# Moving weight sums from GpSimd to VectorE and fetching a stage's raw weights eight deep, in a one-core transformer layer

## The chip, the cores and the metric

The kernel runs on one core of one Trainium2 chip. The metric is the device time of one execution in microseconds (us). The kernel before took 2723.49 us (median of three runs, 2721.57 to 2726.60).

## The reference

One layer over 1024 latent tokens and 256 context tokens, model width 1024, all in fp32:

```python
def ffn_sublayer(h, shift, scale, gate, g, w_in, w_out):
    hn = modulate(rmsnorm(h, g), shift, scale)
    a, b = jnp.split(hn @ w_in, 2, axis=-1)
    y = (jax.nn.silu(a) * b) @ w_out
    return h + 0.5 * gate[:, None, :] * y

# reference(), in its order
h = x + grid_pos_emb(rows)[None];  hc = ctx
mods   = jnp.split(jax.nn.silu(c) @ w_ada + b_ada, 9, axis=-1)
mods_c = jnp.split(jax.nn.silu(c_ctx)[None] @ w_ada + b_ada, 9, axis=-1)
h  = ffn_sublayer(h,  mods[0],   mods[1],   mods[2],   g_ffn1, w_ffn1_in, w_ffn1_out)
hc = ffn_sublayer(hc, mods_c[0], mods_c[1], mods_c[2], g_ffn1, w_ffn1_in, w_ffn1_out)
p_lat = project(h,  mods[3],   mods[4],   g_mix, w_in, PROJ_SIZES)     # q k v gates | o u vs ga gb
p_ctx = project(hc, mods_c[3], mods_c[4], g_mix, w_in, PROJ_SIZES[:4]) # q k v gates
# short convolution and silu on q, k; chunked mLSTM in both directions, started from the context's states
y_lat = merge_branches(p_lat[4:], hlf + hlb, ...)                      # w_branch_a, w_branch_b, w_out
h = h + mods[5][:, None, :] * y_lat
h = ffn_sublayer(h, mods[6], mods[7], mods[8], g_ffn2, w_ffn2_in, w_ffn2_out)
return rmsnorm(h, g_final)
```

The feed-forward width is 2816, so `w_ffn1_in` has 5632 columns: 44 blocks of 128.

## The kernel before

**Products.** Every fp32 operand of a large product is split into a high and a low part: ScalarE casts it to the TensorE's fp32r format (line 145), VectorE subtracts the cast from the original (line 146), and TensorE does three products (high by high, high by low, low by high). So each weight page goes from DRAM to a raw page, through one cast and one subtraction, into a page of pairs, `hl` or `ring`.

**Products with sums.** For the 1024 latent tokens a 2 x 2 block of products is done as seven products of sums and differences of the blocks. The weights' sums are made just before the cast, on the raw page, by one 128x512 addition or subtraction each. Before the change they are done on GpSimd (`G`), in three places: `Pair.load` (lines 1215, 1217, 1218, 1220; 24 pairs of 128 weight columns, four sums each), `Rows.load` (lines 1152 to 1158; 32 sums) and `Stage.preload` through `Gate.presum` (lines 358 and 359; 12 sums for the first three column blocks of each feed-forward's first half).

**Stages**, by the time of the profile: the conditioning's modulation (`adr`, line 827, until 43 us); the context tokens' first half of the first feed-forward ("context stage", 43 to 202, products `pa` and `pb` through `proj` and line 172); the same for latents (the "Gate", `qa` and `qb`, line 396, from 202 to some 650) and its second half (`po`, line 522); the context's second half; then the projections: value rows (`Rows`), k pairs and q pairs (line 1252, 1030 to 1225), the sigmoid pairs for o, ga and gb (1225 to 1470), and so on to the branches, their output and the second feed-forward.

**The context stage.** `Weights` hands out the 44 split pages in order. A page's load is one step: its DMA into one of two `raw` buffers, and its split into one of three `hl` buffers. `W.done()` after each product of 24 matmuls starts the next load. Meanwhile the latents are prepared: addition of the position embedding (`add_pos`, line 876), sums of squares (`Norm.sq`, lines 198 and 199), scaling by the norm (`Norm.inplace`, lines 248 and 249) and the first split factors of the latents (`fa` in `Factors.early`, `fb` and the subtraction of line 295). After each pair of products the gated result is formed and stored (`sil`, `gc`, lines 946 to 950).

**What sets the order.** The program records its operations in the order it is written, and a scheduler of the language then sets each engine's order. The code steers this with a queue `todo` of small steps, which `pump` takes between matmuls: 512 columns of matmul buy one step, less the step's `cost`. A step marked `later` waits, and all behind it, until VectorE's account (`debt`, filled by `dv` with an estimated length of each VectorE operation, and paid off by matmul columns) is below 128. All DMAs of the kernel are issued by SP, in order. In the projections a `Stream` keeps at least four split `ring` pages ahead of TensorE.

**The pairs.** `Pair.load(p)` for p = 1 takes two of four raw pages and starts their DMAs. Each later p does its sums on them in place and hands the page to the cast. The seven products go in the order 1, 7, 2, 4, 5, 6, 3; product 7's result is copied to SBUF by ScalarE as `py` (line 1263), product 1's as `px` (line 1258). For q and k, the convolution's taps are VectorE's lines 1331 and 1333 (tile `cv`), and ScalarE's lines 1330 and 1353. During the sigmoid pairs VectorE also computes the remaining modulation vectors (`adacc`, lines 766 and 768), from weights that come through two buffers `adapg` (DMAs of line 756).

Of the kernel before, what the change touches and what calls it, by code (L numbers as in the profile page):

```python
# [56 lines left out]
def _build(ctx, tc, nc, a, out):  # L57
# [48 lines left out]
    class Weights:  # L106


        def __init__(self, order, name):
            self.c = ExitStack()  # L110
            self.pool = self.c.enter_context(tc.tile_pool(name=name, bufs=1, reuse_waits="tile"))
            self.order = deque(order)
            self.ready = deque()
            self.held = 0

        def load(self):
            n, i, w = self.order.popleft()
            src = a[n][i]
# [5 lines left out]
            self.held += 1  # L124

        def take(self, n, i):
            if not self.ready:
                self.load()
# [56 lines left out]
    class Norm:  # L185
# [5 lines left out]
        def sq(self, d, first=None):  # L191
            nt = self.nt
            if d == 0 if first is None else first:
                self.acc = t2("acc")
                S.activation(self.acc[:, :nt], self.h[d], AF.Square)
            else:
                sq = t2("sq")
                S.activation(sq[:, :nt], self.h[d], AF.Square)
                (self.eng if d % self.alt == 0 else V).tensor_tensor(self.acc[:, :nt], self.acc[:, :nt], sq[:, :nt], ALU.add)
# [46 lines left out]
        def inplace(self, d, sc, sh):  # L246
            t = self.h[d]
            V.scalar_tensor_tensor(t, t, sc[:, d:d + 1], self.rb, ALU.mult, ALU.mult)
            S.activation(t, t, AF.Identity, bias=sh[:, d:d + 1])
# [69 lines left out]
    class Gate:  # L319
# [31 lines left out]
        def presum(self, f, eng):  # L351
# [3 lines left out]
            if eng is V:  # L355
                dv()
                dv()
            eng.tensor_tensor(s1, b1, b2, ALU.add)
            eng.tensor_tensor(b1, a1, b1, ALU.subtract)

        def load(self):
# [4 lines left out]
            else:  # L366
# [4 lines left out]
                if p in (5, 6) and "s1" not in s:  # L371
                    self.presum(f, V)
# [200 lines left out]
    class Stage:  # L573
# [284 lines left out]
    W = Weights([("w1i", f, 1024) for f in range(2 * NF)], "w1")  # L858
# [10 lines left out]
    def add_pos(tb, d):  # L869
        hv = h[tb][d].rearrange("p (r c) -> p r c", c=64)  # L870
# [9 lines left out]
    W.load()  # L880
    W.load()
    apg.append(ada_pages(2))
    W.load()
# [25 lines left out]

    n1 = [Norm(h[tb], 512, V) for tb in range(2)]  # L910
    s0, b0 = smod[:, 0, 0, :], mods[:, 0, 0, :]

    def slow(fn, *args, cost=1024):
        f = it(fn, *args)
        f.cost = cost
        todo.append(f)

    for f in range(NF):
# [15 lines left out]
        if f == 12:  # L934
            A.head()
        if f > 12:
            A.preload()
        wa = W.take("w1i", 2 * f)
# [3 lines left out]
        W.done()  # L942
        proj(pb, wb, hnc)
        W.done()
        sil = t2("sil")[:, :256]
        S.activation(sil, pa, AF.Silu)
        V.tensor_mul(sil, sil, pb)
        g = t2("gc", F32R, (128, 2, 256))
        split(g, sil)
        nc.sync.dma_start(gcsp[f // 2, :, f % 2], g.bitcast(F32))  # L950
# [24 lines left out]
    A.gate(A.F.late(fpage, lambda k: []), tick)  # L975
# [153 lines left out]
    class Rows:  # L1129
# [13 lines left out]
        def load(self, p, k):  # L1143
# [57 lines left out]
    class Pair:  # L1201


        def __init__(self, name, i, emit, ctx_emit=None):
            self.name, self.i, self.emit, self.ctx_emit = name, i, emit, ctx_emit
            self.steps = PSEQ if ctx_emit is None else PSEQ[:1] + (8,) + PSEQ[1:]

        def load(self, p):
            if p == 1:
                self.s = [rawpg() for _ in range(2)]  # L1210
                for j in range(2):
                    nc.sync.dma_start(self.s[j], a[self.name][self.i + j])
            a1, a2, b1, b2 = (self.s[j][:, o * 512:(o + 1) * 512] for j in range(2) for o in range(2))
            if p == 7:
                G.tensor_tensor(b1, a1, b1, ALU.subtract)
            elif p == 5:
                G.tensor_tensor(b2, b2, b1, ALU.subtract)  # L1217
                G.tensor_tensor(a1, a1, b2, ALU.add)  # L1218
            elif p == 3:
                G.tensor_tensor(a2, a2, b2, ALU.subtract)  # L1220
# [66 lines left out]

    def pair_steps(*args):
        pr = Pair(*args)
        for p in pr.steps:  # L1290
# [365 lines left out]

    nvs, barvs = rows_steps("wvs", emit_vs)
# [437 lines left out]
```

## Time and profile before

| | us |
|---|---|
| median of three runs | 2723.49 |
| the profiled execution | 2722.22 |
| span of its trace | 2720.4 |
| TensorE busy | 2661.8 |
| VectorE busy | 1974.2 |
| ScalarE busy | 1085.2 |
| GpSimd busy | 330.0 |

One execution is profiled; its span runs from the first to the last instruction, and its own time is 1.8 us longer. In the rows below, PE is TensorE, PEld its weight loads, DVE VectorE, ACT ScalarE, POOL GpSimd, and SPq the DMA queue of SP. L146 is line 146 of the kernel before. "x24" counts instructions. In the timeline the columns are start, length, engine, line, operation, output and inputs, with the idle time just before and what ended it in brackets. A wait reads: engine, line and tile that waited, what it waited for, total us, times, longest. A group of instructions reads: busy us and mean ns of one, then the idle time before them.

### The profile page before, as it was taken

Reading aid. Unit: us, or ns where it says so; the run is one execution under the profiler, and the core shown is the slowest. Engines: PE = TensorE matmul, PEld = TensorE weight load, DVE = VectorE, ACT = ScalarE, POOL = GpSimd, SP = SyncE. Lnnn points to the kernel's source line nnn. Section 1 sums busy time; section 2 is a strip of 40 time slices with the busy share of each in tenths; the row PEclk is TensorE's granted clock in tenths of the full one; section 3 lists DMA queues with packets and bytes.
Section 4 is the critical chain, followed back from the end, with each engine's and each line's share of the span. In section 5 each row is a group of like instructions: output and inputs, shape, how many; then the busy total and the mean of one; then the engine's idle time right before and its main releaser. Section 6 shows DMA issues by size and latency. Waiting matters only on the chain.

```text
span 2720.4 us, 35602 instructions
## 1 busy us (share of the span) xinstructions
PE 2661.8 (98%) x12734; PEld 2210.9 (81%) x12734; DVE 1974.2 (73%) x3469; ACT 1085.2 (40%) x1862; POOL 330.0 (12%) x354
## 2 busy tenths in 40 slices
PE   8899999999999999999999999999999999999998
PEld 4788888888889878777878888888877888888887
DVE  4787897887969646667665677768468977776755
ACT  3564333334436625444434333112145433333432
POOL 0100000000000122232221315443010000000000
PEclk9999999999999999999999999999999999999999
DMA  8862453449668322237554357547331333337645
GB/s 279 283 192 74 162 173 123 145 151 321 212 215 283 123 78 73 87 109 237 172 171 155 106 187 259 191 168 258 125 132 63 128 136 117 123 121 257 198 159 170
DMA packets 199584, 456.73 MB, mean 168 GB/s; under 512 B 20592, under 2 KB 49008, under 8 KB 199408
## 3 DMA queue, kind: packets, MB, share of 16 engines
q1 hardware_dynamic: 199408, 454.47, 49.7%
q8 instruction: 100, 1.64, 0.2%
q14 instruction: 76, 0.62, 0.1%
HBM read 328.95 MB, written 125.51 MB: 167 GB/s over the span
## 4 chain that ended last, share of the span: by engine, by line
PE 52%; DVE 5%; issue 2%; POOL 1%; DMA 1%; ACT 1%; SPq 0%; POOLq 0%; DVEq 0%; ACTq 0%
PE pq L1252 13%; PE qb L396 10%; PE pt L1720 9%; PE po L522 6%; PE qa L396 5%; PE pr L1171 3%; PE pn L1833 2%; PE pu L1560 2%; PE pn L1831 1%; DVE ring L146 1%; PE pkc L1232 1%; DMA adapg<-in_w_ada_dram 1%; PE pm L1677 1%; POOL rawq L1217 0%; POOL rawq L1218 0%
## 5 line engine op out<-in xcount | busy, mean ns | idle before, releaser
L145 ACT CAST ring<-rawq 128x512 fp32r<-128x512 f32 x432 | 266.6, 620 | 565.5 <-PE qb L396 193.4
L146 DVE TENSOR_TENSOR ring<-rawq,ring 128x512 fp32r<-128x512 f32 x432 | 311.1, 722 | 185.9 <-ACT ring L145 183.6
L522 PE MATMUL po<-gring,wring 128*128 128x512 f32 (+1 forms) x1896 | 425.4, 385 | 0.4 <-ACT wring L145 0.3
L522 PEld LDWEIGHTS po<-gring,wring 128*128 128x128 f32 x1896 | 349.4, 188 | 72.2 <-issue 1.2
L396 PE MATMUL qb<-fc,ring 128*128 128x512 f32 x1440 | 340.0, 390 | 1.1 <-DVE u L417 0.8
L396 PEld LDWEIGHTS qb<-fc,ring 128*128 128x128 f32 x1440 | 269.8, 188 | 58.9 <-DVE u L417 2.3
L396 PE MATMUL qa<-fa,ring 128*128 128x512 f32 x1056 | 253.3, 390 | 0.5 <-ACT ring L145 0.5
L396 PEld LDWEIGHTS qa<-fa,ring 128*128 128x128 f32 x1056 | 197.9, 188 | 42.7 <-ACT ring L145 0.9
L1252 PE MATMUL pq<-fc,ring 128*128 128x512 f32 x864 | 216.4, 399 | 14.4 <-ACT py L1263 9.3
L396 PE MATMUL qb<-fb,ring 128*128 128x512 f32 x984 | 229.8, 389 | 0.0
L396 PEld LDWEIGHTS qb<-fb,ring 128*128 128x128 f32 x984 | 184.6, 188 | 38.4 <-DVE fb L146 0.2
L1252 PEld LDWEIGHTS pq<-fc,ring 128*128 128x128 f32 x864 | 162.1, 190 | 52.3 <-ACT py L1263 11.2
L145 ACT CAST wring<-rw 128x512 fp32r<-128x512 f32 x154 | 95.8, 622 | 227.6 <-PE po L522 192.8
L1720 PE MATMUL pt<-yp,ring 128*128 128x512 f32 x768 | 184.2, 396 | 0.0
L146 DVE TENSOR_TENSOR wring<-rw,wring 128x512 fp32r<-128x512 f32 x154 | 105.6, 686 | 94.2 <-ACT wring L145 94.0
L1720 PEld LDWEIGHTS pt<-yp,ring 128*128 128x128 f32 x768 | 144.1, 188 | 29.3
L1252 PE MATMUL pq<-fa,ring 128*128 128x512 f32 x576 | 142.6, 396 | 0.2 <-ACT px L1258 0.2
L1252 PE MATMUL pq<-fb,ring 128*128 128x512 f32 x576 | 137.6, 393 | 0.4 <-DVE mods L783 0.4
L1252 PEld LDWEIGHTS pq<-fa,ring 128*128 128x128 f32 x576 | 108.5, 191 | 24.2 <-ACT px L1258 1.1
L1252 PEld LDWEIGHTS pq<-fb,ring 128*128 128x128 f32 x576 | 107.7, 188 | 23.1 <-PE pu L1601 0.7
L768 DVE SCALAR_TENSOR_TENSOR adacc<-adapg,sc,adacc 128x512 f32<-128x512 f32 x140 | 110.6, 803 | 14.4 <-DMA adapg<-in_w_ada_dram 13.5
L145 ACT CAST ring<-rawt 128x512 fp32r<-128x512 f32 x64 | 39.5, 619 | 186.3 <-PE pt L1720 172.4
(341 smaller groups left out, 4241.8 us busy)
## 6 DMA issues: line engine op xcount, KB each, us to landing
adapg<-in_w_ada_dram SPq DMA_DIRECT2D x144, 256.0 KB, 4.0
fsp<-fhl SPq DMA_DIRECT2D x66, 512.0 KB, 2.7
gring<-fsp SPq DMA_DIRECT2D x66, 512.0 KB, 3.8
raw<-in_w1i_dram SPq DMA_DIRECT2D x44, 512.0 KB, 4.4
graw<-fsp SPq DMA_DIRECT2D x88, 256.0 KB, 3.6
rawq<-in_w1i_dram SPq DMA_DIRECT2D x38, 512.0 KB, 4.2
rawq<-in_w2i_dram SPq DMA_DIRECT2D x38, 512.0 KB, 3.3
fsp<-x SPq DMA_DIRECT2D x66, 256.0 KB, 2.0
```

The source lines that it names most:

```text
L145: S.copy(hl[:, 0, :], src)
L146: V.tensor_sub(hl[:, 1, :], src, hl[:, 0, :].bitcast(F32))
L396: T.matmul(pt, hl[:, x, sl], pages[p][k][:, y, :], start=first and i == 0, stop=i == 11, skip_group_check=not first)
L522: T.matmul(pt[:, cs], w[:, x, sl], g[:, y, cs], start=grp and kp == 0 and i == 0, stop=kp == NFP - 1 and i == 2, skip_group_check=not grp)
L768: eng.scalar_tensor_tensor(acc, pgt, sc2[:, q, k:k + 1], acc, ALU.mult, ALU.add)
L1171: T.matmul(self.pt[m], pg[:, x, sl], hl[:, y, :], start=first and k == 0 and i == 0, stop=k == 3 and i == 2, skip_group_check=not first)
L1232: T.matmul(self.cp[:, o:o + 256], hl[:, x, k * 128:(k + 1) * 128], hnc[kc][:, y, :], start=p == 1 and k == 0 and i == 0, stop=p in (2, 4) ...
L1252: T.matmul(pt, hl[:, x, k * 128:(k + 1) * 128], pg[k][:, y, :], start=first and k == 0 and i == 0, stop=k == 3 and i == 2, skip_group_chec ...
L1560: T.matmul(pu[:, 0:257], ksl[:, kt * 128:(kt + 1) * 128], wv, start=True, stop=True)
L1677: T.matmul(pm[:, n * 128:(n + 1) * 128], vnp_[:, half * 4 + n, :], wsr_[:, half * 4 + n, :], start=True, stop=True)
L1720: T.matmul(pt, hl[:, x, k * 128:(k + 1) * 128], pg[:, y, :], start=kh + k + i == 0, stop=kh == 1 and k == 3 and i == 2)
L1833: T.matmul(pn[:, 0:257], qi[:, c_, :], self.C[d][:, c_, :], start=False, stop=c_ == 1)
```

## The change

1. **Sums.** All 140 sums of `Pair.load`, `Rows.load` and `presum` go from GpSimd to VectorE. `preload` no longer does the `presum` at once but puts it into `todo`, as `later`, at cost 512.
2. **Pairs' pages.** A pair starts the DMAs of the next pair's raw pages at its own third step, instead of at the next pair's first.
3. **Context weights.** Fetching and splitting are taken apart. Raw pages come from the pool `hn`, eight deep (`wraw`; the first four, of which one is new ahead of the last modulation page, from another pool); split pages `hl` are four deep instead of three.
4. **Gated results.** `gate_c` of a column block is recorded after the next block's first product instead of right behind its own.
5. **Latents' preparation.** The steps `add_pos`, `sq`, `inplace` and `early` cost 512 instead of 1024, are `later`, and charge VectorE's account. Twelve empty steps stand between the norm's root and its use. The scaling of the second half of the latents (eight `inplace`) goes to the Gate's list of steps.
6. **First ring pages.** The Gate's first three ring pages are loaded before the context stage's last two products.

```diff
         def load(self):
-            n, i, w = self.order.popleft()
-            raw = self.pool.tile([128, w], F32, name="raw", tag="raw", bufs=2)
-            nc.sync.dma_start(raw, src)
-            hl = self.pool.tile([128, 2, w], F32R, name="hl", tag="hl", bufs=3)
+            n, i, raw = self.raws.popleft()
+            hl = self.pool.tile([128, 2, 1024], F32R, name="hl", tag="hl", bufs=self.depth)
             split(hl, raw)
             self.ready.append((n, i, hl))
...
+        def fetch(self, page):
+            n, i, w = self.order.popleft()
+            raw = page()
+            nc.sync.dma_start(raw, a[n][i])
+            self.raws.append((n, i, raw))
...
-        def done(self, n=1):
-            self.held -= n
-            while self.order and self.held < 3:
+        def done(self, page):
+            if self.raws:
                 self.load()
+            while self.order and len(self.raws) < self.ahead:
+                self.fetch(page)
...
                 if i:
-                    self.q.presum(f, G)
+                    fn = it(self.q.presum, f)
+                    fn.cost, fn.later = 512, True
+                    todo.append(fn)
...
-    W = Weights([("w1i", f, 1024) for f in range(2 * NF)], "w1")
+    W = Weights([("w1i", f, 1024) for f in range(2 * NF)], "w1", 4, 8)
...
+    def wraw():
+        return hnp.tile([128, 1024], F32, name="wraw", tag="pg1", bufs=8)
...
+    for _ in range(W.ahead):
+        W.fetch(wraw)
...
-                slow(add_pos, tb, f - 2)
-                slow(n1[tb].sq, f - 2)
+                slow(add_pos, tb, f - 2, cost=512, later=True)
+                slow(n1[tb].sq, f - 2, cost=512, later=True)
...
-            todo.extend([n1[0].rstd, nop, n1[1].rstd, nop, n1[0].bcast, n1[1].bcast])
+            todo.extend([n1[0].rstd, n1[1].rstd] + [nop] * 12 + [n1[0].bcast, n1[1].bcast] + [nop] * 4)
             for d in range(NKT):
-                slow(n1[0].inplace, d, s0, b0)
-                slow(A.F.early, fpage, 1 if d < 4 else 2, d % 4)
-            for d in range(NKT):
-                slow(n1[1].inplace, d, s0, b0)
+                slow(n1[0].inplace, d, s0, b0, cost=512, later=True)
+                slow(A.F.early, fpage, 1 if d < 4 else 2, d % 4, cost=512, later=True)
...
+        if f == NF - 1:
+            A.q.ring = lambda: hnpage(1, "ring0")
+            for _ in range(HEAD):
+                A.q.load()
+            A.q.ring = A.ring
...
         proj(pa, wa, hnc)
-        W.done()
+        if gated is not None:
+            gated()
+        W.done(wraw)
         proj(pb, wb, hnc)
-        W.done()
+        W.done(wraw)
+        gated = it(gate_c, f, pa, pb)
...
-    A.gate(A.F.late(fpage, lambda k: []), tick)
+    A.gate(A.F.late(fpage, lambda k: [it(n1[1].inplace, k, s0, b0)]), tick)
...
             if p == 1:
-                self.s = [rawpg() for _ in range(2)]
+                self.fetch()
+            elif p == self.steps[2] and self.next is not None:
+                self.next.fetch()
...
             if p == 7:
-                G.tensor_tensor(b1, a1, b1, ALU.subtract)
+                V.tensor_tensor(b1, a1, b1, ALU.subtract)
             elif p == 5:
-                G.tensor_tensor(b2, b2, b1, ALU.subtract)
-                G.tensor_tensor(a1, a1, b2, ALU.add)
+                V.tensor_tensor(b2, b2, b1, ALU.subtract)
+                V.tensor_tensor(a1, a1, b2, ALU.add)
             elif p == 3:
-                G.tensor_tensor(a2, a2, b2, ALU.subtract)
+                V.tensor_tensor(a2, a2, b2, ALU.subtract)
```

Apart from the context stage, TensorE's order is the same but for one swap of small products. Three places show how other engines' orders change. The changed kernel has other line numbers: its cast and subtraction are lines 149 and 150.

The first place is SP's queue at the head of the context stage. `raw` and `wraw` are pages of the first feed-forward's weights, `h` the latents' pages, `hsp` and `gcsp` stores. Before:

```order
L120 DMA raw<-in_w1i_dram 128x1024
L820 DMA adapg<-in_w_ada_dram 128x2x256 x8
L885 DMA cst<-in_cst_dram 128x512
L886 DMA pos<-in_pos_dram 128x320
L921 DMA h<-in_xT_dram 128x512 x2
L120 DMA raw<-in_w1i_dram 128x1024 x2
L921 DMA h<-in_xT_dram 128x512 x4
L855 DMA hsp<-h 128x512
```

Now:

```order
L122 DMA wraw<-in_w1i_dram 128x1024 x2
L827 DMA adapg<-in_w_ada_dram 128x2x256 x8
L903 DMA cst<-in_cst_dram 128x512
L904 DMA pos<-in_pos_dram 128x320
L122 DMA wraw<-in_w1i_dram 128x1024 x8
L951 DMA h<-in_xT_dram 128x512 x2
L122 DMA wraw<-in_w1i_dram 128x1024 x2
L951 DMA h<-in_xT_dram 128x512 x2
```

One more weight page stands ahead of the last modulation page, and eight more ahead of the latents' first pages.

The second place is ScalarE's queue over one q pair (`cv` the convolution's tile; `px`, `py` and `pre` copies out of PSUM; `ring` the cast of a weight page). Before:

```order
L1258 COPY px<-pq 128x512
L145 CAST ring<-rawq 128x512
L1353 ACTIVATE cv<-cv 128x1024
L1263 COPY py<-pq 128x512
L145 CAST ring<-rawq 128x512
L1353 ACTIVATE cv<-cv 128x1024
L1297 COPY pre<-pq 128x512
```

Now:

```order
L1297 COPY px<-pq 128x512
L1397 ACTIVATE cv<-cv 128x1024
L1302 COPY py<-pq 128x512
L149 CAST ring<-rawq 128x512 x2
L1397 ACTIVATE cv<-cv 128x1024
L1341 COPY pre<-pq 128x512
```

The cast that stood ahead of the copy `py` now stands behind it, next to the one that followed.

The third place is VectorE's queue in the same pair. Before:

```order
L1331 SCALAR_TENSOR_TENSOR cv<-pre,vec,cv 128x1023
L146 TENSOR_TENSOR ring<-rawq,ring 128x512
L1333 SCALAR_TENSOR_TENSOR cv<-pre,vec,cv 128x1023
L1331 SCALAR_TENSOR_TENSOR cv<-pre,vec,cv 128x1023
L146 TENSOR_TENSOR ring<-rawq,ring 128x512
L1333 SCALAR_TENSOR_TENSOR cv<-pre,vec,cv 128x1023
L146 TENSOR_TENSOR ring<-rawq,ring 128x512 x3
L1265 TENSOR_TENSOR py<-py,pq 128x512
```

Now:

```order
L1375 SCALAR_TENSOR_TENSOR cv<-pre,vec,cv 128x1023
L150 TENSOR_TENSOR ring<-rawq,ring 128x512
L1377 SCALAR_TENSOR_TENSOR cv<-pre,vec,cv 128x1023
L1255 TENSOR_TENSOR rawq<-rawq 128x512
L1375 SCALAR_TENSOR_TENSOR cv<-pre,vec,cv 128x1023
L1256 TENSOR_TENSOR rawq<-rawq 128x512
L1377 SCALAR_TENSOR_TENSOR cv<-pre,vec,cv 128x1023
L150 TENSOR_TENSOR ring<-rawq,ring 128x512 x2
L1258 TENSOR_TENSOR rawq<-rawq 128x512
L150 TENSOR_TENSOR ring<-rawq,ring 128x512 x2
L1304 TENSOR_TENSOR py<-py,pq 128x512
```

The two sums of product 5 (lines 1255 and 1256) stand between the convolution's taps, each behind one, and the sum of product 3 (line 1258) two subtractions later.

More of the change, by code (lines that the diff above doesn't have):

```diff
@@ L106, in _build, with __init__ @@
     class Weights:
-        def __init__(self, order, name):
+        def __init__(self, order, name, depth, ahead):
             self.c = ExitStack()
@@ L196, in sq @@
             else:
+                dv(nt)
                 sq = t2("sq")
@@ L246, in inplace @@
         def inplace(self, d, sc, sh):
+            dv(self.nt)
             t = self.h[d]
@@ L354, in presum @@
             s1 = self.s[f]["s1"] = self.sums("s1")
[L355 to L359, printed above, removed]
+            dv()
+            dv()
+            V.tensor_tensor(s1, b1, b2, ALU.add)
+            V.tensor_tensor(b1, a1, b1, ALU.subtract)
         def load(self):
@@ L879, in _build @@
     apg = [ada_pages(0), ada_pages(1)]
-    W.load()
-    W.load()
+    for _ in range(2):
+        W.fetch(wfirst)
+        W.load()
     apg.append(ada_pages(2))
-    W.load()
+    for _ in range(2):
+        W.fetch(wfirst)
+        W.load()
     apg.append(ada_pages(3))
@@ L908, in _build, with slow, gate_c @@
             prs.append(ada_mm(apg[3]))
+    for _ in range(W.ahead):
+        W.fetch(wraw)
     n1 = [Norm(h[tb], 512, V) for tb in range(2)]
     s0, b0 = smod[:, 0, 0, :], mods[:, 0, 0, :]
-    def slow(fn, *args, cost=1024):
+    def slow(fn, *args, cost=1024, later=False):
         f = it(fn, *args)
-        f.cost = cost
+        f.cost, f.later = cost, later
         todo.append(f)
+    def gate_c(f, pa, pb):
+        sil = t2("sil")[:, :256]
+        S.activation(sil, pa, AF.Silu)
+        V.tensor_mul(sil, sil, pb)
+        g = t2("gc", F32R, (128, 2, 256))
+        split(g, sil)
+        nc.sync.dma_start(gcsp[f // 2, :, f % 2], g.bitcast(F32))
+    gated = None
     for f in range(NF):
@@ L1206, in __init__, with fetch @@
             self.steps = PSEQ if ctx_emit is None else PSEQ[:1] + (8,) + PSEQ[1:]
-        def load(self, p):
-            if p == 1:
+            self.s, self.next = None, None
+        def fetch(self):
+            if self.s is None:
                 self.s = [rawpg() for _ in range(2)]
@@ L1286, in rows_steps @@
         return n, r.bar
+    last = [None]
     def pair_steps(*args):
         pr = Pair(*args)
+        if last[0] is not None:
+            last[0].next = pr
+        last[0] = pr
         for p in pr.steps:
@@ L1655, in emit_vs @@
         nc.sync.dma_start(vnsp[i, :, j * 512:(j + 1) * 512], t)
+    last[0] = None
     nvs, barvs = rows_steps("wvs", emit_vs)
```

35 lines of the change are left out of this document (18 added, 17 removed).

## The prediction

> **What bounds the kernel now.** I read the page's busy line first, then TensorE's waits by stage, and then single stretches of the timeline.
>
> ```profile
> PE 2661.8 (98%) x12734; PEld 2210.9 (81%) x12734; DVE 1974.2 (73%) x3469; ACT 1085.2 (40%) x1862; POOL 330.0 (12%) x354
> ```
>
> TensorE sets the time nearly everywhere, so the change can only win back TensorE's gaps. The view of busy time by stretch shows which stages have any. Its columns are: stretch, length, busy time of TensorE, of its weight loads, VectorE, ScalarE and GpSimd, granted clock, DMA share, GB/s.
>
> ```profile
> 43.00:57.00 14.00, 13.31 (x93) 12.64 (x92) 11.42 (x30) 6.48 (x13) 2.37 (x3) 0.88 0.47 162
> 57.00:105.00 48.00, 42.16 (x329) 40.12 (x330) 34.39 (x49) 24.39 (x41) 0.00 (x0) 1.00 0.87 278
> 105.00:202.00 97.00, 87.76 (x675) 83.03 (x673) 82.11 (x138) 59.82 (x94) 10.10 (x6) 0.98 0.67 220
> 202.00:1100.00 898.00, 894.95 (x4284) 746.75 (x4285) 698.38 (x1180) 383.43 (x655) 44.87 (x36) 1.00 0.49 164
> 1150.00:1200.00 50.00, 43.98 (x191) 35.42 (x190) 34.47 (x37) 22.72 (x33) 18.62 (x11) 1.00 0.27 93
> 1235.00:1500.00 265.00, 261.33 (x1139) 212.98 (x1140) 175.87 (x267) 106.68 (x206) 69.42 (x52) 0.99 0.56 177
> ```
>
> The holes are in the context stage (43 to 202: 6 us and then 9 us of idle) and in the q pairs (6 us in 50). From 202 to 1100 there is nothing to win: 3 us in 898.
>
> The context stage's waits, and the pace that TensorE keeps when nothing is late:
>
> ```profile
> ACT hl L145 <- DMA raw<-in_w1i_dram: 22.9, 17, 3.0
> PE pb L172 <- DVE hl L146: 8.0, 12, 1.5
> PE pa L172 <- DVE hl L146: 3.6, 3, 2.2
> PE pb L172 <- ACT hl L145: 2.7, 5, 0.6
> ```
> ```profile
> 66.05 3.04 PE L172 MATMUL pa<-hnc,hl 128*128 128x256 f32 x24
> 68.92 0.46 PE L172 MATMUL pb<-hnc,hl 128*128 128x256 f32 x2
> 70.14 2.90 PE L172 MATMUL pb<-hnc,hl 128*128 128x256 f32 x22 [0.76 <-DVE hl L146]
> ```
>
> A product of 24 matmuls starts at 66.05 and the next at 68.92: 2.87 us, so 0.12 us a matmul. TensorE waits for the split weights (subtraction L146 after cast L145), and the cast waits for the raw page's DMA.
>
> **The context stage.** Why the page is late follows from three durations:
>
> ```profile
> L146 DVE TENSOR_TENSOR hl<-raw,hl 128x1024 fp32r<-128x1024 f32 x40 | 50.4, 1261 | 18.0 <-ACT hl L145 17.9
> L145 ACT CAST hl<-raw 128x1024 fp32r<-128x1024 f32 x39 | 40.8, 1046 | 23.3 <-DMA raw<-in_w1i_dram 22.9
> raw<-in_w1i_dram SPq DMA_DIRECT2D x44, 512.0 KB, 4.4
> ```
>
> With two raw buffers, a buffer goes round in landing 4.4, cast 1.05 and subtraction 1.26 = 6.7 us: 3.36 us per page at best, against 2.87 that TensorE needs. Forty pages at 3.36 are 134 us of the 145 after 57. Eight buffers take the landing out of the round, and four split ones instead of three let a late subtraction pass unseen. What is late next?
>
> ```profile
> L217 PE MATMUL rb<-diag,ones 128*128 128x512 f32 x4 | 2.0, 591 | 0.0
> L204 PE MATMUL p<-ones,acc 128*128 128x1 f32 x16 | 1.8, 245 | 0.0
> L248 DVE SCALAR_TENSOR_TENSOR h<-h,smod,rb 128x512 f32<-128x512 f32 x16 | 11.7, 738 | 0.0
> 20.00:30.00 10.00, 10.00 (x33) 3.06 (x32) 4.79 (x18) 2.09 (x2) 0.00 (x0) 1.00 1.07 370
> ```
>
> TensorE: its 1056 matmuls (44 products of 24) take 126.7 us from 43.1 on, and with the latents' norm matmuls, 2.0 + 1.8, the floor is 173.6. VectorE: its busy time in 43 to 202 is 11.42 + 34.39 + 82.11 = 127.9 us. The change moves some of the latents' preparation towards the Gate, though the scheduler still puts most of that ahead of the last split; the moved weight sums (six at 0.68, priced below, for three heads) may come in, 4.1 us. So 124 to 132 us, and VectorE's floor ends at 167 to 175, the same as TensorE's. Two engines that are both full don't meet without queueing. DMA: 14 x 162 + 48 x 278 + 97 x 220 KB are 36.9 MB; at 278 GB/s that is 133 us, until 176. So all three floors lie at 167 to 176, and the old end at 202.
>
> To the floor of 173.6 I add: 1.4 for one more 512 KB page ahead of the last modulation page (at the 370 GB/s of 20 to 30); 2.8 that is already lost at the start (14.0 less 93 x 0.12), since the context's normalised chunks come one by one; 1.5 for the latents' norm matmuls, which now stand earlier on TensorE against a VectorE that is not early; 4 for queueing on VectorE, over a quarter of the 14.3 of waits on L146 and L145 quoted above. That ends the stage at 183.3 instead of 202, and I take **-18.5 us**. Bounds: -28 (floor alone) and -4.5 (the DMA goes on at the 239 GB/s that the two rows from 57 have together, 154 us, until 197.5).
>
> **The Gate's start** takes up to eight scalings of 0.74 us and the sums: some 7 to 10 us of VectorE. Between 210 and 240 it has room:
>
> ```profile
> 210.00:240.00 30.00, 30.00 (x134) 24.86 (x133) 13.75 (x21) 11.27 (x19) 0.00 (x0) 1.00 0.00 2
> ```
>
> I take 0; without the 16 us of idle there it would cost the 7 to 10, for there TensorE has none to spare.
>
> **The q pairs.** One loss in full, and the sum of the five:
>
> ```profile
> 1190.03 1.28 DVE L1331 SCALAR_TENSOR_TENSOR cv<-pre,vec,cv 128x1023 f32<-128x1023 f32 x1 [0.72 <-ACT cv L1330]
> 1192.00 2.27 POOL L1217 TENSOR_TENSOR rawq<-rawq 128x512 f32<-128x512 f32 x1 [3.83 <-DVE ring L146]
> 1193.03 2.32 DVE L1331 SCALAR_TENSOR_TENSOR cv<-pre,vec,cv 128x1023 f32<-128x1023 f32 x1
> 1194.34 2.15 POOL L1218 TENSOR_TENSOR rawq<-rawq 128x512 f32<-128x512 f32 x1
> 1196.53 0.62 ACT L145 CAST ring<-rawq 128x512 fp32r<-128x512 f32 x1 [4.41 <-POOL rawq L1218]
> 1198.01 0.56 ACT L1263 COPY py<-pq 128x512 f32<-128x512 f32 x1
> 1198.63 4.61 PE L1252 MATMUL pq<-fc,ring 128*128 128x512 f32 x12 [2.13 <-ACT py L1263]
> ...
> PE pq L1252 <- ACT py L1263: 9.3, 5, 2.1
> ```
>
> GpSimd's two sums for product 5 end at 1196.5. ScalarE's cast of them waits 4.41 us, and behind it in ScalarE's queue stands the copy `py`, which frees the PSUM bank that TensorE needs. The change does two things here: in ScalarE's new order `py` stands ahead of that cast, and the sums go to VectorE, where the operation of that shape costs 0.68:
>
> ```profile
> L1331 DVE SCALAR_TENSOR_TENSOR cv<-pre,vec,cv 128x1023 f32<-128x1023 f32 x10 | 18.0, 1799 | 2.9 <-ACT cv L1330 2.9
> L1299 DVE TENSOR_TENSOR pre<-px,pq 128x512 f32<-128x512 f32 x9 | 6.1, 680 | 0.4 <-PE pq L1252 0.3
> ```
>
> L1331 ran ten times in the 100 us of that view, twice a pair: 20 us a pair. A pair's four sums add 4 x 0.68 = 2.7 us to VectorE, which is idle for 15.5 of the 50 us from 1150, so 6.2 a pair. The sums stand between the convolution's operations and delay the cast by at most 1.28 + 2.32, less than the 4.41 it waits now. Were that slack not there, a pair would pay the 2.7 instead of winning the 1.9 of today's wait. I take **-9.0** of the 9.3; bounds -9.3 and -5 (the split of product 5 takes over half of the wait).
>
> [...]
>
> **The sigmoid pairs and the rest.** The other 114 sums (140 less five pairs' and the first heads') cost VectorE 78 us, over stages in which GpSimd was not what TensorE waited for:
>
> ```profile
> ACT ring L145 <- POOL rawq L1218: 37.0, 11, 5.5
> DVE adacc L768 <- DMA adapg<-in_w_ada_dram: 11.5, 14, 1.6
> ```
>
> The casts waited for GpSimd 11 times between 1225 and 1480, up to 5.5 us, yet TensorE was idle for only 3.7 of the 265 us from 1235: the split ring is deep enough. Against that, sums now stand in VectorE's queue among the `adacc` operations, which wait for their DMAs. VectorE's load in 1235 to 1500 grows by 12 x 4 x 0.68 = 32.6 to 208.5 of 265. Loading the next pair's pages earlier removes no TensorE wait that I find. I take **0**, bounds -4 and +8 (three late sums at the price below).
>
> **Sum.** -18.5 - 9.0 = -27.5 on the profiled execution's 2722.2 (span 2720.4 and 1.8 around it): 2694.7. That execution lies 1.3 under the median of the three runs, 2723.5, so **2696**.
>
> **Rivals.** *The first stage stays bound by transfer or VectorE* (20%). For it: 0.87 of DMA time taken in 57 to 105, and VectorE's floor as long as TensorE's. Against: 278 GB/s there and only 162 just before show that the two buffers leave bandwidth idle. It gives -4.5 - 9.0 and 2710.
>
> *VectorE is full* (10%). In the Gate it already is:
>
> ```profile
> 250.00:300.00 50.00, 50.00 (x223) 41.39 (x222) 49.67 (x83) 21.52 (x37) 0.00 (x0) 1.00 0.48 163
> 1235.00:1245.00 10.00, 9.26 (x33) 7.41 (x34) 9.48 (x14) 4.68 (x9) 2.91 (x2) 0.83 0.71 222
> ```
>
> If such stretches as the second hold a quarter of the 32.6 us of sums and pass them to TensorE, 8 are lost, and 2704. [...] Here VectorE is saturated in the Gate, where no pair sum lies, and at 34.47 of 50 in the q pairs.
>
> *Slower: sums behind a DMA wait* (5%). One place shows the price:
>
> ```profile
> 1231.67 0.49 DVE L766 TENSOR_SCALAR adacc<-adapg,sc 128x512 f32<-128x512 f32 x1 [1.82 <-DMA adapg<-in_w_ada_dram]
> 1232.68 2.41 DVE L768 SCALAR_TENSOR_TENSOR adacc<-adapg,sc,adacc 128x512 f32<-128x512 f32 x2
> 1235.01 0.67 DVE L1265 TENSOR_TENSOR py<-py,pq 128x512 f32<-128x512 f32 x1
> 1235.74 0.50 PE L1252 MATMUL pq<-fc,ring 128*128 128x512 f32 x1 [2.54 <-DVE py L1265]
> ```
>
> An `adacc` that waits holds what stands behind it, and TensorE loses 2.54. GpSimd's sums were outside that queue; now 36 pre-cast steps of the 12 sigmoid pairs are in it. From 11 late ones the gain of 27.5 is gone; with every second one late, 18 x 2.54 = 46 are lost, and 2742. Against it: the ring's slack of 5.5, above.
>
> **How the numbers follow.** The forecast has 60% (own range 2687 to 2703), 5% go to a first stage at its floor (2685), and the rivals take 20, 10 and 5%. The range of 8 in 10 is 2685 to 2712. About 0.2%, 5.4 us, is what this kernel's times tell from no change. Faster by more: the forecast, the floor, the first two rivals, less some mixtures, 92%; within it 4%; slower 4%.
>
> **What would show it.** In the new profile: the first stage's end (the first `qa` matmul) near 184, with TensorE's waits for `hl` below 7 us and the casts' waits for raw pages nearly gone; no TensorE wait for `py` in the q pairs; GpSimd down by 140 instructions. I am wrong if `qa` starts after 195, if TensorE waits for `ring` in the pairs, or if waits for `adacc`'s neighbours pass 10 us.

## The result, and the profile after

The changed kernel takes 2679.71 us (median of four runs, 2677.91 to 2681.91) against 2723.30 for the kernel before on the same chip. The ratio is 0.9839, with a 95% interval of 0.9822 to 0.9856. The forecast was 2696 with a range of 2685 to 2712: the direction was right, and the gain, 43.6 us, is more than half again the 27.5 that was forecast, which puts the time 5.3 us below the range.

The page's busy line of the changed kernel answers to the one shown of before: 2679.1 us of span against 2720.4, GpSimd down from 330 to 127 us.

```profile
PE 2645.9 (99%) x12734; PEld 2206.2 (82%) x12734; DVE 2004.1 (75%) x3609; ACT 1086.1 (41%) x1862; POOL 127.2 (5%) x214
```

TensorE's order is the same apart from the context stage, so the two traces can be laid side by side by the first matmul of each stage:

| part | before, us | after, us | difference |
|---|---|---|---|
| until the first context matmul | 43.1 | 41.8 | -1.3 |
| context stage, to the first `qa` matmul | 159.0 | 140.8 | -18.2 |
| Gate | 422.3 | 421.8 | -0.5 |
| its second half (`po`) | 213.2 | 216.0 | +2.8 |
| the four q pairs | 86.6 | 76.2 | -10.5 |
| the eleven pairs behind them, of the sigmoid's twelve | 238.0 | 230.1 | -7.9 |
| all else | 1558.2 | 1552.4 | -5.8 |

The stretches of busy time, the same columns as in the prediction (length; TensorE, weight loads, VectorE, ScalarE, GpSimd; clock, DMA share, GB/s), show the start of the context stage, the rest of it, the q pairs and the sigmoid pairs of the changed kernel:

```profile
42.00:57.00 15.00, 14.94 (x121) 14.44 (x120) 8.49 (x25) 8.06 (x16) 2.19 (x3) 1.00 0.64 240
57.00:182.60 125.60, 119.97 (x975) 118.43 (x974) 114.02 (x194) 80.30 (x130) 0.00 (x0) 0.99 0.75 268
1105.00:1182.00 77.00, 77.00 (x341) 63.76 (x340) 59.81 (x81) 40.58 (x56) 0.00 (x0) 1.00 0.33 117
1182.00:1412.00 230.00, 227.90 (x1003) 185.91 (x1002) 179.60 (x293) 102.43 (x202) 0.00 (x0) 1.00 0.59 189
```

From 57 us on TensorE is idle for 5.6 us of the context stage, instead of 15.1, and in the q pairs not at all. What it still waits for in the context stage is new. The larger of the two waits below (us in total, times, longest) is for ScalarE's `sil` (line 941), and the timeline shows how the first of its two cases comes about:

```profile
PE pa L176 <- ACT sil L941: 4.0, 2, 2.0
PE rb L222 <- DVE rs_y L751: 1.7, 1, 1.7
```
```profile
90.84 1.04 ACT L149 CAST hl<-wraw 128x1024 fp32r<-128x1024 f32 x1 [1.82 <-PE pb L176]
91.79 0.62 ACT L203 ACTIVATE sq<-h 128x512 f32<-128x512 f32 x1
...
92.32 0.36 ACT L941 ACTIVATE sil<-pa 128x256 f32<-128x256 f32 x1
92.74 1.46 PE L176 MATMUL pa<-hnc,hl 128*128 128x256 f32 x10 [1.98 <-ACT sil L941]
```

`sil` reads the result of an earlier product, and the next product waits until it has been read. In ScalarE's queue it stands behind a cast that waits until TensorE is done with `pb`. So TensorE stops for ScalarE, which had just stopped for TensorE.

### The profile page after: what moved, and what is told of

Same layout as the page of the kernel before. It is cut to its first block, busy times and chain, and to the rows that moved or that the text cites. A ratio compares the mean times of both kernels' runs of the same rounds, so it can differ in the third digit from the quotient of the medians.

```text
span 2679.1 us, 35551 instructions
## 1 busy us (share of the span) xinstructions
PE 2645.9 (99%) x12734; PEld 2206.2 (82%) x12734; DVE 2004.1 (75%) x3609; ACT 1086.1 (41%) x1862; POOL 127.2 (5%) x214
## 4 chain that ended last, share of the span: by engine, by line
PE 87%; DVE 6%; DMA 3%; issue 2%; ACT 1%; SPq 0%; POOL 0%; POOLq 0%; DVEq 0%; ACTq 0%
PE qb L401 19%; PE po L527 13%; PE pq L1291 13%; PE qa L401 10%; PE pt L1765 10%; PE pr L1202 6%; PE pa L176 2%; PE pb L176 2%; PE pc L1073 2%; PE pn L1878 2%; PE pu L1604 2%; PE adr L834 1%; DVE ring L150 1%; PE pkc L1271 1%; PE pn L1876 1%
## 5 line engine op out<-in xcount | busy, mean ns | idle before, releaser
L150 DVE TENSOR_TENSOR ring<-rawq,ring 128x512 fp32r<-128x512 f32 x432 | 295.8, 689 | 132.3 <-ACT ring L149 130.6
L775 DVE SCALAR_TENSOR_TENSOR adacc<-adapg,sc,adacc 128x512 f32<-128x512 f32 x140 | 102.6, 745 | 9.3 <-DMA adapg<-in_w_ada_dram 8.5
```

Source lines behind the costliest of these rows:

```text
L150: V.tensor_sub(hl[:, 1, :], src, hl[:, 0, :].bitcast(F32))
L775: eng.scalar_tensor_tensor(acc, pgt, sc2[:, q, k:k + 1], acc, ALU.mult, ALU.add)
```

## The experiments

### Which part of the change gives what

Four kernels undo or do one part alone. Two leave the context stage as before and move all sums of `Pair.load` and `Rows.load`, without and with the earlier fetch of pages; of the pairs' sums two are shown:

```diff
-                G.tensor_tensor(b2, b2, b1, ALU.subtract)
-                G.tensor_tensor(a1, a1, b2, ALU.add)
+                V.tensor_tensor(b2, b2, b1, ALU.subtract)
+                V.tensor_tensor(a1, a1, b2, ALU.add)
...
```

> The kernel before with only the 96 Pair and 32 Rows sums on VectorE; nothing else of the change. Theory A (GpSimd's sums were what held ScalarE's and VectorE's queues): the q pairs lose no TensorE time on py (9.3 us of waits before) and the slow clock after 1196 goes too (about 1.7 us), and in the sigmoid pairs adacc (L768) gets shorter than its 892 ns, so that most of the 7.9 us won there come back: 18 to 20 us less, 2704 +- 2. Theory B (the sigmoid pairs were won by fetching the next pair's pages earlier): only the q pairs' 10.5 us, 2713.

> The kernel before with the Pair and Rows sums on VectorE and the earlier fetch, without the context stage's parts. Theory A: as sums_only, within 1 us. Theory B: sums_only less 7 to 8 us. In sum with stage_only's gain it should give the whole change's 43.6 us.

One does the earlier fetch alone:

```diff
...
+            elif p == self.steps[2] and self.next is not None:
+                self.next.fetch()
...
```

> The kernel before with only the earlier fetch of the next pair's pages; all sums stay on GpSimd. Theory A: no gain, within 2 us of before, the q pairs' waits for py still about 9 us. Theory B: the sigmoid pairs win most of 7.9 us, adacc's waits for its DMA fall from 11.5 to about 5.4 us, and the time is about 2716.

And one takes both out of the changed kernel, so that the context stage's parts are left:

> The changed kernel with all sums back on GpSimd and without the earlier fetch of pairs' pages, so only the context stage's parts. If the parts add up, the first qa matmul comes at 182 to 184 us and everything behind the Gate is as before: 2723.3 - 19.5 = 2704, with the projections' losses of before (10.5 in the q pairs, 8 in the sigmoid pairs) still there. If the context stage alone also moves later stages, it lies more than 2 us away from that.

| kernel | median, us | ratio to before (95%) | first `qa` |
|---|---|---|---|
| sums_only | 2701.0 | 0.9913 (0.9898 to 0.9928) | 201.6 |
| sums_prefetch | 2699.7 | 0.9908 (0.9893 to 0.9923) | 202.4 |
| prefetch_only | 2722.2 | 1.0003 (0.9992 to 1.0013) | 204.6 |
| stage_only | 2704.2 | 0.9925 (0.9908 to 0.9941) | 183.4 |

Before was 2723.9 in these runs. The earlier fetch does nothing by itself. The sums give 22.9 us, with the fetch 24.2, and the context stage 19.7; 24.2 + 19.7 = 43.9 is the whole change's 43.6. Theory A was right, though its 2704 was 3 us too high, and theory B fell: the gain in the sigmoid pairs belongs to the sums. In the profile of sums_only the q pairs are shorter by 10.5 us, the eleven pairs by 8.4, the k pairs by 1.9, and the rest comes in smaller pieces. TensorE's waits for `py` in the pairs, first with the sums moved, then with the fetch alone, show it; `DVE py` is VectorE's addition to `py`, `ACT py` ScalarE's copy. With the fetch alone, `adacc` waits for its DMA as long (11.2 us) as before (11.5), where theory B had 5.4:

```profile
PE pq L1252 <- DVE py L1265: 1.3, 2, 1.1
```
```profile
DVE adacc L768 <- DMA adapg<-in_w_ada_dram: 11.2, 12, 2.6
...
PE pq L1259 <- ACT py L1270: 10.1, 5, 2.6
...
PE pq L1259 <- DVE py L1272: 5.8, 5, 2.6
```

### Why the sigmoid pairs gained

Either GpSimd's results had come late, or GpSimd's work beside VectorE had slowed VectorE's own operations. The first of two kernels puts GpSimd's work back without anybody needing it:

```diff
...
+            for _ in range({7: 1, 5: 2, 3: 1}.get(p, 0)):
+                G.tensor_tensor(gscr, hl[:, 0, :].bitcast(F32), hl[:, 1, :].bitcast(F32), ALU.add)
```

> The changed kernel with four extra GpSimd additions of 128x512 per pair that read a split ring page and write a scratch page nobody reads; VectorE's and ScalarE's orders are the changed kernel's. It does more work than the reference asks for. Theory A1 (GpSimd beside VectorE slows VectorE's own operations, and that was the sigmoid pairs' loss): adacc goes from 745 back to about 800 ns on the whole and to 890 in the sigmoid pairs, the convolution's L1375 from about 1.3 to 1.8 us, waits of TensorE for py come back there, and the time grows by 3 to 8 us. Theory A2 (what counted was GpSimd's results coming late): same time within 1.5 us.

The second puts two of a pair's four sums back:

```diff
             if p == 7:
-                V.tensor_tensor(b1, a1, b1, ALU.subtract)
+                G.tensor_tensor(b1, a1, b1, ALU.subtract)
...
             elif p == 3:
-                V.tensor_tensor(a2, a2, b2, ALU.subtract)
+                G.tensor_tensor(a2, a2, b2, ALU.subtract)
```

> The changed kernel with the sums of products 7 and 3 of each pair back on GpSimd, those of product 5 on VectorE; ScalarE's order keeps py ahead of the cast. My step of the prediction (the cast of product 5 held py): the q pairs keep their whole gain of 10.5 us. With A1 half of the sigmoid pairs' 7.9 us is lost, with A2 none.

gdummy took 2688.7 us (0.9866, 0.9850 to 0.9882), 9.0 us over the changed kernel by the medians, though the spans of the two profiled executions lie only 4.5 apart; p5v took 2681.5 (0.9837, 0.9823 to 0.9852). VectorE's groups over the same eleven pairs, in order: before, changed, gdummy, p5v (busy us and mean ns of one; then the idle time before):

```profile
L146 DVE TENSOR_TENSOR ring<-rawq,ring 128x512 fp32r<-128x512 f32 x80 | 61.4, 770 | 45.4 <-ACT ring L145 45.1
L768 DVE SCALAR_TENSOR_TENSOR adacc<-adapg,sc,adacc 128x512 f32<-128x512 f32 x56 | 49.8, 889 | 12.4 <-DMA adapg<-in_w_ada_dram 11.5
```
```profile
L150 DVE TENSOR_TENSOR ring<-rawq,ring 128x512 fp32r<-128x512 f32 x80 | 54.4, 686 | 16.8 <-ACT ring L149 16.4
L775 DVE SCALAR_TENSOR_TENSOR adacc<-adapg,sc,adacc 128x512 f32<-128x512 f32 x56 | 41.9, 748 | 6.2 <-DMA adapg<-in_w_ada_dram 5.4
```
```profile
L150 DVE TENSOR_TENSOR ring<-rawq,ring 128x512 fp32r<-128x512 f32 x81 | 68.0, 848 | 9.1 <-ACT ring L149 8.9
L775 DVE SCALAR_TENSOR_TENSOR adacc<-adapg,sc,adacc 128x512 f32<-128x512 f32 x56 | 49.5, 884 | 4.9 <-DMA adapg<-in_w_ada_dram 4.2
```
```profile
L775 DVE SCALAR_TENSOR_TENSOR adacc<-adapg,sc,adacc 128x512 f32<-128x512 f32 x56 | 44.3, 790 | 10.5 <-DMA adapg<-in_w_ada_dram 9.7
```

With GpSimd busy beside it, VectorE's `adacc` takes 884 to 889 ns instead of 748, whether the sums are needed or not. The eleven pairs take 236.7 us in gdummy, so 6.6 of the 7.9 us are lost again. TensorE is idle there for 7.0 us, against 2.1 in the changed kernel, and most of that is for `py`. Its waits in the eleven pairs, before (two rows), changed and gdummy:

```profile
PE pq L1252 <- DVE py L1265: 5.1, 4, 2.5
PE pq L1252 <- ACT py L1263: 1.7, 1, 1.7
...
PE pq L1291 <- DVE py L1304: 1.1, 2, 0.9
...
PE pq L1294 <- DVE py L1307: 4.7, 4, 1.8
```

In gdummy the order of VectorE and ScalarE is the changed kernel's, and neither of them waits for GpSimd in this stage. So GpSimd's work alone, with a result that nobody reads, costs this time, and A2 is refuted for this stage. But gdummy is not the kernel before: its VectorE does the sums too and is busy for 206 of the 236.7 us, against 167 of 238.0. What happened before can be read from its own timeline, at one of the four waits for VectorE's `py`:

```profile
1274.64 1.29 POOL L1218 TENSOR_TENSOR rawq<-rawq 128x512 f32<-128x512 f32 x1
1275.56 2.62 DVE L768 SCALAR_TENSOR_TENSOR adacc<-adapg,sc,adacc 128x512 f32<-128x512 f32 x2 [1.60 <-DMA adapg<-in_w_ada_dram]
1275.89 1.75 POOL L1220 TENSOR_TENSOR rawq<-rawq 128x512 f32<-128x512 f32 x1
1278.10 0.67 DVE L1265 TENSOR_TENSOR py<-py,pq 128x512 f32<-128x512 f32 x1
```

Two `adacc` take 2.62 us here, against 1.50 for two of 748 ns, and the addition to `py` stands right behind them. At the other three waits the two take 2.41, 2.60 and 2.61 us. Over the four waits that is 4.3 us too long, against 5.1 that TensorE waits; the time for which such `adacc` wait for their own DMA, 1.60 us here, is not counted. So most of the gain in the sigmoid pairs comes from GpSimd no longer slowing VectorE. The 1.7 us for ScalarE's `py` are another matter: this wait, at 1221.7, stands behind a cast of product 5, as in the q pairs.

The q pairs kept their 76.2 us in gdummy and in p5v. So neither a slower VectorE nor the sums of products 7 and 3 counted there, and what is left is the sums of product 5 with their cast ahead of `py`, as the prediction had it. Whether the cast's place in ScalarE's queue or the lateness of the sums made the loss is not separated: in sums_only, gdummy and p5v both are mended at once. p5v lost 0.8 us of 7.9 in the eleven pairs, not half as A1 had it: `adacc` at 790 ns still leaves enough. Kernels with all sums on VectorE differ by 2.6 us there (227.5 to 230.1), so p5v's loss may be none. Why gdummy's median lies further above the changed kernel than its profile was not traced.

Gdummy shows the slowing for `adacc` (748 to 884 ns) and for the subtraction of the ring (686 to 848 ns). The convolution's L1375, which was slowed before (L1331 there, 1.80 us), stayed at 1.28 in gdummy; whether the additions ran at other moments there was not shown. In p5v it was the convolution's other line, L1377, that took 1.80 us.

### What the context stage needed

The first kernels took the stage's parts away one by one, by the last two numbers of `Weights` (split pages, pages fetched ahead: raw2 has 4 and 2 as shown, hl3 3 and 8, raw2_hl3 3 and 2) and by the marks of the preparation's four steps (prep_old; raw2_hl3_prep has both):

```diff
-    W = Weights([("w1i", f, 1024) for f in range(2 * NF)], "w1", 4, 8)
+    W = Weights([("w1i", f, 1024) for f in range(2 * NF)], "w1", 4, 2)
```
```diff
-                slow(add_pos, tb, f - 2, cost=512, later=True)
+                slow(add_pos, tb, f - 2)
...
```

> The changed kernel with two raw pages fetched ahead instead of eight. If the two buffers' round (landing 4.4 + cast 1.05 + subtraction 1.26 = 3.36 us a page) set the context stage, qa starts at 195 to 202 us instead of 182.6. If the depth of the split pages or the marks of the latents' preparation did it, qa stays below 188.

> The changed kernel with three split pages instead of four (eight raw ones). Theory S (the fourth split page gives the slack that VectorE's late subtractions need): the waits of TensorE for hl come back and qa comes after 188 us. Theory P (the latents' preparation, halved in cost and held back by VectorE's account, no longer stands in front of the subtractions): qa stays below 185.

> The changed kernel with the preparation's steps at their old cost of 1024 and not marked as later (VectorE's account is still charged). Theory P: qa comes after 190, with waits for hl. Theory S: below 186.

> The changed kernel with two raw and three split pages, as many as before the change; the preparation's marks, the deferred gating and the early ring pages stay. Theory S, or raw and split depth together: qa at 195 or later. Theory P: below 185; then no depth was needed.

> Two raw and three split pages, and the preparation's steps at their old cost and not later. If depth and marks are the whole gain, qa comes at 198 to 203, as before the change; what is missing to that belongs to the separate fetch, the deferred gating and the early ring pages.

| kernel (one execution each; of the changed kernel the median time) | first `qa`, us | time, us |
|---|---|---|
| changed kernel | 182.6 | 2679.7 |
| raw2 | 175.1 | 2671.3 |
| hl3 | 187.2 | 2679.9 |
| prep_old | 184.1 | 2679.6 |
| raw2_hl3 | 177.7 | 2671.0 |
| raw2_hl3_prep | 176.6 | 2672.9 |

Nothing that was taken away brought the stage's old end of 202 back, and three of the kernels are faster than the changed one. That speaks against theory S, against theory P, and, at first sight, against the raw buffer's round of the prediction. But raw2 tests less than its expectation says: it fetches two pages ahead, but the pool keeps eight pages, so a DMA never waits for a page. Two more kernels separate the buffers from the lead. The first really has as few as before, with three split pages and fetches two ahead:

```diff
-        return hnp.tile([128, 1024], F32, name="wraw", tag="pg1", bufs=8)
+        return W.pool.tile([128, 1024], F32, name="wraw", tag="raw", bufs=2)
```

> The changed kernel with really as few buffers as before: two raw pages in the stage's own pool (raw2 and raw2_hl3 fetched two ahead but kept eight buffers, so that a DMA never waited for one) and three split pages. Theory R (my prediction's: a raw buffer's round of landing, cast and subtraction is longer than the two products that it has): waits of TensorE for hl and of the casts for the page's DMA return, and qa comes at 192 to 202 us. Theory F (what counts is that a page's DMA is recorded one load before its split, not the buffers): qa stays below 183.

The second keeps the eight pages, leaves out the eight fetches ahead of the stage, and records fetch and split as one step again:

```diff
         def done(self, page):
-            if self.raws:
-                self.load()
-            while self.order and len(self.raws) < self.ahead:
+            if self.order:
                 self.fetch(page)
+                self.load()
...
```

> The changed kernel with its eight raw buffers and four split ones, but each page fetched and split in one step, as before the change, so that the cast stands in ScalarE's queue right when its DMA is issued. Theory R: qa below 183, since the buffers are there. Theory F: the casts wait 20 us or more for DMAs again, with the gating and the preparation behind them, and qa comes after 190.

buf2_hl3 put `qa` at 199.4 us (2692.4), joined at 176.7 (2672.3). buf2_hl3 differs from raw2_hl3, at 177.7, only in the number of raw pages, and 22 us lie between them. First the waits over the stage and the row of a page's DMA (its last figure the time to landing) of buf2_hl3, then the same of raw2_hl3:

```profile
ACT hl L149 <- DMA wraw<-in_w1i_dram: 31.8, 24, 3.3
...
PE pa L176 <- DVE hl L150: 5.9, 10, 0.9
PE pb L176 <- ACT hl L149: 5.4, 3, 2.2
```
```profile
wraw<-in_w1i_dram SPq DMA_DIRECT2D x38, 512.0 KB, 4.5
```
```profile
ACT hl L149 <- DMA wraw<-in_w1i_dram: 1.9, 2, 1.0
```
```profile
wraw<-in_w1i_dram SPq DMA_DIRECT2D x33, 512.0 KB, 6.1
```

With two pages the round of 4.5 + 1.05 + 1.25 us, 3.4 a page, is longer than TensorE's 2.87, and TensorE waits. With eight pages a landing may take 6.1 us and the casts wait 1.9 us for it in all. So theory R holds and theory F falls: the raw buffers are the context stage's gain. All other parts together leave 2.7 us between buf2_hl3 and the 202.1 of before.

For the fourth split page and the preparation's marks these single executions show no gain. hl3 and prep_old end the stage later than the changed kernel, by 4.6 and 1.5 us, but not because of waits for `hl` (0.6 us and none): behind a wait for `sil` TensorE runs for 10 us at half clock in hl3, and prep_old has as many waits for `sil` (both three, 4.6 us). The row of hl3:

```profile
110.20:120.20 10.00, 10.00 (x49) 10.00 (x48) 4.91 (x25) 1.98 (x3) 0.00 (x0) 0.50 0.41 122
```

raw2_hl3 ends the stage 2.6 us later than raw2, with 0.8 us of waits for `hl`, and takes the same time in all (2671.0 and 2671.3).

### Why the changed kernel still waits, and a faster one

```diff
-        if gated is not None:
-            gated()
...
-        gated = it(gate_c, f, pa, pb)
+        gate_c(f, pa, pb)
```

> The changed kernel with gate_c recorded right behind its own two products, as before the change. The changed kernel's two waits of TensorE for sil (2.0 us each, at 92 and 100) come from the deferral if they are gone here; then qa comes some 4 to 6 us earlier, with the slow clock after the second one. If VectorE's queue needs the deferral, new waits for hl take more than that and qa comes after 183.

> The changed kernel with fetches two pages ahead (eight buffers) and the gating recorded right behind its products. Each alone took away TensorE's two waits for sil and brought qa to 175.1 and 177.3 instead of 182.6. If both cure the same two waits, together they give no more: qa at 174 to 177 and 2669 to 2672 us. If they cure different ones, 2664 or less.

> The changed kernel with fetches two pages ahead, timed: 2671 +- 2, that is 8 us under the changed kernel and clear of its interval, if the one look was typical; 2679 if it was chance.

undefer took 2669.1 us in one execution, with `qa` at 177.3; raw2_t, timed, 2670.7 us (0.9808, 0.9794 to 0.9823), with `qa` at 174.9. In neither does TensorE wait for `sil`. Both changes at once gave 2676.5 (0.9822, 0.9801 to 0.9843; its four runs lie between 2669.4 and 2678.1), with `qa` at 181.1, where 174 to 177 was expected. So the two don't add up; that they harm each other isn't shown, since this interval overlaps that of raw2_t. In its profile TensorE hardly waits in the stage (1.0 us for `hl`), but more than five microseconds run at half clock:

```profile
105.00:110.00 5.00, 4.37 (x30) 4.37 (x31) 3.24 (x11) 2.83 (x4) 0.00 (x0) 0.80 1.03 406
110.00:115.00 5.00, 5.00 (x26) 5.00 (x26) 4.93 (x25) 1.32 (x2) 0.00 (x0) 0.52 0.89 291
```

raw2_t, with one number changed, is the fastest timed kernel: 9.0 us under the changed kernel by the medians, though the two intervals just touch. All kernels with fetches eight ahead and the deferred gating have the two waits of 1.98 us; none of those with two ahead or with the gating in place has them.

## Why the prediction was wrong

**The context stage: right in mechanism, the end in part by luck.** The forecast was `qa` at 183.3, and it came at 182.6. The raw buffer's round is the cause (buf2_hl3), and the floor was nearly right: in raw2_t TensorE is never idle in the stage, which takes 132.6 us against the floor's 130.5. The additions to the floor were less good, and that they still fit the end is luck. The 1.4 for the page ahead of the last modulation page and the 2.8 of the start did not come: the stage began 1.3 us earlier, by chance, as kernels with the same start begin it between 41.2 and 43.7 us, and TensorE is full from 42 to 57. The 4 for queueing on VectorE came as two waits of 1.98 for `sil` and a slow clock behind the second (1.5). The slow clock need not come: p5v has the same two waits, keeps its full clock and takes 139.3 us for the stage instead of 140.8. The rows behind the second wait, changed and p5v:

```profile
100.70:104.90 4.20, 4.17 (x23) 4.17 (x24) 3.09 (x6) 0.94 (x2) 0.00 (x0) 0.64 0.48 157
...
101.36:105.56 4.20, 4.18 (x34) 4.18 (x35) 3.08 (x6) 1.89 (x4) 0.00 (x0) 1.00 0.45 147
```

The 1.5 for the norm matmuls came as 1.7 for `rs_y`.

**VectorE's floor and the marks: irrelevant.** I reasoned that VectorE was as full as TensorE and would leave a rest of 4 us of waits for `hl`. No such wait is left in the changed kernel, and the kernels without the marks end the stage about as early.

**The q pairs: right in mechanism, too small.** -9.0 was forecast for five waits, and -10.5 measured in the four q pairs, where four of the five lie; the fifth is the 1.7 us at 1221.7, in the first sigmoid pair. The waits for `py` are gone, and so is what followed one of them: 1.5 us lost to a slow clock (0.52 from 1199.40 to 1202.80), which the term left out.

**The sigmoid pairs: the step that failed.** "I take 0, bounds -4 and +8" was -7.9, or -6.2 without that fifth wait. One error was in reading: "idle for only 3.7 of the 265 us" counts from 1235, where the longest wait, until 1235.74, was nearly over. From 1211 on it is twice that:

```profile
1211.00:1449.00 238.00, 230.56 (x1003) 187.06 (x1003) 167.24 (x241) 101.11 (x200) 67.88 (x48) 0.99 0.57 182
```

The larger error was the mechanism. The step looked for a queue in which GpSimd stood and found that the casts' waits for it cost nothing. That was right, and it was not the point. The rows quoted for the q pairs showed the point (L1331 at 1.28 us, and at 2.32 beside GpSimd's L1217), and the sum has no term for it. In the sigmoid pairs such slowing is on the path. The rows quoted for the slower rival show it: L768 took 2.41 us for two at 1232.68, beside GpSimd's sums, and the addition to `py` stood behind it while TensorE waited for 2.54. What I priced as a danger of the change was mostly a cost that the change removes. On VectorE, 56 `adacc` of 889 less 748 ns are 7.9 us. That this equals the stage's gain is chance: eight of the 56 stand right in front of the four late additions to `py`.

**The rest.** The context stage's end came 1.0 us more forward than the 18.5 taken. The Gate, `po` and "all else" sum to -3.5, where 0 was forecast; 1.8 of it lies in one place, a wait of 1.27 us for a split page at 1988 that the kernel before has. I have no cause for these parts and did not test them. The +2.8 in `po` did not come back in gdummy (213.5 there) and isn't a trait of the change: over the kernels here `po` takes 212.5 to 216.0 us. The remaining 2.3 us are between the profiled executions (41.3 apart, by their spans) and the medians (43.6).

**The rivals.** A first stage bound by transfer or VectorE did not come: DMAs moved 268 GB/s over the stage. VectorE was not too full for the sums. The sums did not get stuck behind `adacc`: its waits for DMA even fell.

## What to carry to other kernels

Before leaving work on GpSimd because TensorE does not wait for GpSimd, look at what VectorE's operations take with and without GpSimd beside them (here `adacc` 884 and 748 ns): the price may be paid on VectorE and be seen as a wait for VectorE. For a stream of weights, work out the round of a raw buffer (landing, cast, subtraction) per page against the time in which a page is used, and add buffers until it is shorter; more lead than that can rearrange other engines' queues, as the two waits for `sil` of 1.98 us show. And a test that takes buffers away has to take the buffers, not the number of pages asked for ahead.

## What was unexpected of the hardware

Some waits of TensorE cost more than their length. In the kernel before, a wait at 1196 was followed by 3.4 us at half clock, and one of about the same length at 1174 was not:

```profile
1174.00:1178.00 4.00, 1.87 (x9) 1.23 (x8) 2.31 (x3) 2.57 (x4) 2.24 (x2) 1.00 0.14 56
1178.00:1182.00 4.00, 4.00 (x19) 3.31 (x18) 1.97 (x3) 2.67 (x4) 0.00 (x0) 1.00 0.78 215
...
1196.00:1199.40 3.40, 1.27 (x6) 0.75 (x5) 2.22 (x3) 2.57 (x4) 1.72 (x2) 1.00 0.14 57
1199.40:1202.80 3.40, 3.40 (x10) 2.59 (x9) 1.36 (x3) 2.05 (x3) 0.00 (x0) 0.52 0.67 194
```

A gap in TensorE's pace is the time from one matmul's start to the next, less what this takes when nothing is late (0.12 or 0.23 us). In the traces of before and after, six gaps are between 2.1 and 2.8 us long. Within 1.6 us of the end of four of them a stretch at half clock (0.50) begins: before at 138, 1200 and 1237 us, behind waits that the change removes, and after at 102 us. None follows the other two, which end at 1177 us before and at 93 us after. Each of these four stretches was 3.4 us long; in the one at 1200 us a product of 12 matmuls took 4.61 us, against 3.04 for the one at 1177. That of hl3, above, was 10 us long. Of the gaps between 1.2 and 2.0 us in the two traces only the last of each, 1.9 us long, is followed within 6 us by a half clock (from 2712 us before, 2672 after). Slow stretches also came without a gap: at 49 and 1019 us before and at 1000 us after, with no gap over 0.3 us in the 6 us ahead, and in raw2_undefer at 108 us (TensorE's longest wait in that stage is 0.8 us). What sets them off stays open.
